# One 512-column product over both input parts in place of two of 256 columns, in a split-precision transformer trunk

## The chip, the cores and the metric

The kernel runs on one core of a Trainium2 chip, as one program. The metric is the device time of one execution in microseconds, median of several. TensorE (PE) does the products, VectorE (DVE) and ScalarE (ACT) read their sums out of PSUM, GpSimd (POOL) and the DMA queues do the rest.

## The reference

One inference step of a four-layer decoder trunk with a width of 1024, for 512 prompt tokens and 8 sample tokens that share all weights. Layers 0 and 3 mix tokens with a diagonal state space model (S5), layer 1 with stick-breaking attention, layer 2 with a chunked gMLP; after each mixer comes a SwiGLU feed-forward sub-layer with 2816 hidden columns, and around every sub-layer an RMS norm. Everything is float32.

```
for i in range(DEPTH):                        # 4
    xpn = rms_norm(xp, norm_mix_pre[i])       # and the same for the sample tokens
    op = mixer(xpn)                           # S5, attention, gMLP, S5
    xp = xp + rms_norm(op, norm_mix_post[i])
    h = rms_norm(xp, norm_ffn_pre[i])
    gate, up = jnp.split(h @ w_ffn_in[i], 2, axis=-1)
    xp = xp + rms_norm((jax.nn.silu(gate) * up) @ w_ffn_out[i], norm_ffn_post[i])
```

## The kernel before

Activations lie with features on the partitions and the 520 tokens (512 and 8) as columns. A dense product gives one output tile m of 128 features by 520 tokens, summed over k, the tiles of 128 input features (8 of them, or 6 in the first chunk of the feed-forward output). For precision near float32 each weight and each input is cut in two parts of type float32r: a high part (`wh`, `xh`), which ScalarE copies, and the low part that is left (`wl`, `xl`), a difference on VectorE or GpSimd. Three products are summed: wh by xh, wh by xl, wl by xh.

The 520 columns are two halves, HA = 256 and HB = 264. `mm` (line 225) issues one step of k: for each half the two products with `wh` (lines 231 and 232), then for each half the one with `wl` (line 234), so six products for both halves. The sums of an item lie in a pair of PSUM banks, a tile of 1024 columns from `pair`, of which there are three; HA goes to columns 256 to 511, the end of the first bank, HB to 512 to 775, the second.

`full` (line 245) goes over items (an item is one output tile m with a function that evicts it), both halves together, one item after the other or a group of two or three with k outside. Weights are loaded two items ahead: a DMA on the SP queue into `raw`, the cast to `wh` on ScalarE (line 207), the difference `wl` on VectorE (line 208). `split` (line 265) runs a sub-layer's first products (`lead`) and its last ones, one half after the other; it calls `mm` with one half. The last items of a feed-forward sub-layer and of attention's and gMLP's output are two in one group of `full` and then six in `split`.

Evictions: the feed-forward gate is lines 1551 to 1553, its up part line 1562 and then `hilo` (lines 379 and 380), its output line 1574; S5's gate is line 977 (sigmoid on ScalarE) and its value line 984; attention's q, k, v are lines 1341, 1350 and 1358; the output of attention and gMLP is lines 322 and 1409. In attention, line 1225 is a scan on VectorE. Two tasks use the ring `pn` of two buffers of 264 columns: `turn`, the norm between sub-layers, and attention's sample task, for its losses (`em`) and its sums (`accv`, lines 1130 to 1137).

The order of the work is written out by `pe`, which counts a modelled time of the products and lets waiting tasks in when they are due; on each engine a scheduler orders the instructions by this order and by what is ready.

## Time and profile before

| | |
|---|---|
| median of 3 runs | 2789.01 us (2787.88 to 2795.05) |
| span of the profiled execution | 2783.3 us |
| TensorE, weight loads | busy 2563.5 us (92%), 2458.0 us (88%) |
| VectorE | busy 1584.0 us (57%) |
| ScalarE | busy 1007.4 us (36%) |
| mean granted clock of TensorE | 0.953 |

The profile is one execution of the program on the chip. Its times are in us, those marked as a mean are ns; an engine is named PE, PEld (TensorE's weight loads), DVE, ACT, POOL or SP, and L231 is line 231 of the kernel. A row names what an instruction writes and reads, as out<-in. Products are pipelined: their durations overlap, so their pace is read from their starts.

### The profile page before, as it was taken

To read this page: it belongs to the slowest core of one execution; us is meant where nothing else is said; L and a number is where in the kernel's file an instruction comes from. 1 tells how busy PE (TensorE), PEld (TensorE's weight loads), DVE (VectorE), ACT (ScalarE), POOL (GpSimd) and SP (SyncE) were. 2 spreads that over 40 slices of the span, in tenths; PEclk is the share of its full clock that TensorE was granted. 3 is DMA by queue.
4 is the path that set the end of the run, shared out by engine and by line. 5 is a ranking of instruction groups with operands and counts; after the bars stand their busy time and mean duration, and the time that the engine had idled before them with its cause. 6 is when DMAs were issued, how large, how long until landed. Compare 5 with 4: busy or idle time off the path is not lost.

```text
span 2783.3 us, 49827 instructions
## 1 busy us (share of the span) xinstructions
PE 2563.5 (92%) x20826; PEld 2458.0 (88%) x20826; DVE 1584.0 (57%) x2668; ACT 1007.4 (36%) x1685; POOL 609.4 (22%) x598
## 2 busy tenths in 40 slices
PE   7769999999898889999998899999998679999998
PEld 6659999999886659999998899999997669999998
DVE  8883643434669975534347666443447864634344
ACT  5443432222346463332223534322223433432221
POOL 5661300000538821200003203000016640300000
PEclk8879999999899989999998999999998889999999
DMA  4533133332346742233324331333322514233331
GB/s 116 144 93 89 57 99 104 93 93 70 111 130 214 228 130 85 75 101 91 92 84 81 99 92 54 110 95 93 93 67 55 143 50 126 65 101 92 91 92 47
DMA packets 476544, 274.49 MB, mean 99 GB/s; under 512 B 51912, under 2 KB 458720, under 8 KB 476320
## 3 DMA queue, kind: packets, MB, share of 16 engines
q1 hardware_dynamic: 467104, 237.76, 30.3%
q0 software_dynamic: 9216, 33.56, 3.6%
q8 instruction: 164, 2.69, 0.4%
q14 instruction: 60, 0.49, 0.1%
HBM read 253.60 MB, written 17.66 MB: 97 GB/s over the span
## 4 chain that ended last, share of the span: by engine, by line
PE 68%; DVE 17%; DMA 3%; ACT 3%; issue 3%; POOL 2%; SPq 0%; ACTq 0%; DVEq 0%; POOLq 0%
PE pp L231 22%; PE pp L232 21%; PE pp L234 21%; DVE m L1225 2%; DVE wl L208 1%; DVE pn L409 1%; DVE x L411 1%; DVE hm L827 1%; DVE xl L394 1%; POOL kp L1089 1%; DVE o L817 1%; DVE zs L1092 1%; DMA rot<-rotd 1%; POOL x L411 1%; DVE o L815 1%
## 5 line engine op out<-in xcount | busy, mean ns | idle before, releaser
L231 PE MATMUL pp<-xh,wh 128*128 128x264 f32 (+1 forms) x4480 | 1217.4, 290 | 36.6 <-ACT xh L393 6.9
L232 PE MATMUL pp<-xl,wh 128*128 128x264 f32 (+1 forms) x4480 | 1216.8, 288 | 10.3 <-DVE xl L394 10.3
L234 PE MATMUL pp<-xh,wl 128*128 128x264 f32 (+1 forms) x4480 | 999.5, 287 | 13.5 <-POOL wl L208 7.4
L231 PEld LDWEIGHTS pp<-xh,wh 128*128 128x128 f32 x4480 | 860.1, 192 | 48.0 <-issue 18.2
L232 PEld LDWEIGHTS pp<-xl,wh 128*128 128x128 f32 x4480 | 861.3, 192 | 14.7 <-DVE xl L394 13.4
L207 ACT ACTIVATE wh<-raw 128x1024 fp32r<-128x1024 f32 (+1 forms) x376 | 390.5, 1042 | 1156.6 <-PE pp L232 873.7
L234 PEld LDWEIGHTS pp<-xh,wl 128*128 128x128 f32 x4480 | 745.1, 192 | 17.9 <-POOL wl L208 7.9
L208 DVE TENSOR_TENSOR wl<-raw,wh 128x1024 fp32r<-128x1024 f32 (+1 forms) x346 | 432.7, 1252 | 292.6 <-ACT wh L207 283.2
L232 PE MATMUL pp<-hl,wh 128*128 128x256 f32 (+1 forms) x1408 | 377.3, 283 | 0.0
L231 PE MATMUL pp<-hh,wh 128*128 128x256 f32 (+1 forms) x1408 | 376.0, 283 | 0.0
L234 PE MATMUL pp<-hh,wl 128*128 128x256 f32 (+1 forms) x1408 | 314.4, 282 | 0.0
L208 POOL TENSOR_TENSOR wl<-raw,wh 128x1024 fp32r<-128x1024 f32 x30 | 71.9, 2402 | 1050.6 <-ACT wh L207 1013.9
L232 PEld LDWEIGHTS pp<-hl,wh 128*128 128x128 f32 x1408 | 265.3, 188 | 0.0
L231 PEld LDWEIGHTS pp<-hh,wh 128*128 128x128 f32 x1408 | 265.0, 188 | 0.0
L234 PEld LDWEIGHTS pp<-hh,wl 128*128 128x128 f32 x1408 | 231.3, 188 | 0.0
L1551 DVE TENSOR_TENSOR tg<-pp,rs 128x520 f32<-128x520 f32 (+2 forms) x100 | 62.5, 631 | 236.6 <-PE pp L234 236.5
L1562 DVE TENSOR_TENSOR tg<-pp,tg 128x520 f32<-128x520 f32 (+2 forms) x96 | 62.6, 652 | 222.6 <-PE pp L234 222.0
L1574 DVE TENSOR_TENSOR op<-pp,op 128x520 f32<-128x520 f32 (+2 forms) x88 | 48.4, 550 | 191.9 <-PE pp L234 191.9
L326 POOL TENSOR_TENSOR acc<-acc,s 128x256 f32<-128x256 f32 (+1 forms) x96 | 83.3, 867 | 74.5 <-ACT s L322 72.5
L394 DVE SCALAR_TENSOR_TENSOR xl<-x,gt,xh 128x264 fp32r<-128x264 f32 (+1 forms) x128 | 86.5, 689 | 3.5 <-ACT xh L393 2.9
L393 ACT ACTIVATE xh<-x,gt 128x264 fp32r<-128x264 f32 (+1 forms) x128 | 62.7, 504 | 57.7 <-POOL x L411 33.4
L1070 POOL MEMSET zs<- 128x28 f32 x1 | 0.1, 121 | 339.3 <-PE pp L234 339.3
(332 smaller groups left out, 2879.1 us busy)
## 6 DMA issues: line engine op xcount, KB each, us to landing
raw<-in_w_ffn_in_dram SPq DMA_DIRECT2D x176, 512.0 KB, 3.8
raw<-in_w_ffn_out_dram SPq DMA_DIRECT2D x64, 512.0 KB, 3.9
raw<-in_w_ssm_glu_dram SPq DMA_DIRECT2D x32, 512.0 KB, 4.6
raw<-in_w_ffn_out_dram SPq DMA_DIRECT2D x32, 384.0 KB, 3.4
raw<-in_w_sb_qkv_dram SPq DMA_DIRECT2D x24, 512.0 KB, 4.1
raw<-in_w_ssm_in_dram SPq DMA_DIRECT2D x16, 512.0 KB, 4.4
wn<-dk SPq DMA_DIRECT2D x128, 64.0 KB, 2.5
raw<-in_w_cm_in_dram SPq DMA_DIRECT2D x16, 512.0 KB, 4.1
```

Source lines behind the costliest of these rows:

```text
L207: nc.scalar.activation(wh[:, :nk], raw[:, :nk], AF.Copy)
L208: (nc.gpsimd if self.edge & WLP else nc.vector).tensor_tensor(wl[:, :nk], raw[:, :nk], wh[:, :nk], op=ALU.subtract)
L231: nc.tensor.matmul(ps(*h), lhsT=wh[:, k, :], rhs=xh[:, h[0]:h[1]], start=first, stop=False)
L232: nc.tensor.matmul(ps(*h), lhsT=wh[:, k, :], rhs=xl[:, h[0]:h[1]], start=False, stop=False)
L234: nc.tensor.matmul(ps(*h), lhsT=wl[:, k, :], rhs=xh[:, h[0]:h[1]], start=False, stop=last)
L326: i = (nc.gpsimd if pool else nc.vector).tensor_tensor(acc[0][:, c0:c1], acc[0][:, c0:c1], sq[:, :n], op=ALU.add)
L393: nc.scalar.activation(xs[k][0][:, c0:c1], self.x[k][:, c0:c1], AF.Copy, scale=g)
L394: nc.vector.scalar_tensor_tensor(xs[k][1][:, c0:c1], self.x[k][:, c0:c1], g, xs[k][0][:, c0:c1], op0=ALU.mult, op1=ALU.subtract)
L411: add.tensor_tensor(self.x[k][:, c0:c1], self.x[k][:, c0:c1], t[:, :n], op=ALU.add)
L1225: v.tensor_tensor_scan(m[:, a:b][:, ::-1], m[:, a:b][:, ::-1], e[:, a:b][:, ::-1], 0.0, op0=ALU.add, op1=ALU.add)
L1551: v.tensor_tensor(g, ps(c0, c1), rs[:, c0:c1], op=ALU.mult)
L1562: v.tensor_tensor(t, ps(c0, c1), t, op=ALU.mult)
```

## The change

In `full`, and there alone, the two products of a step with `wh` on HA become one of 512 columns: its input is both parts of HA's 256 input columns (the low part first), its output the whole first bank, the low sum in columns 0 to 255 and the high sum in 256 to 511. The product with `wl` on HA adds to the high sum, as before. So a step has five products. When an item is done, ScalarE copies its low sum to a buffer of the ring `pn`, VectorE adds it to the high sum in PSUM, and the eviction follows as it was. To make both parts one input, `xh` and `xl` become the two halves of one tile of [128, 2, 520], and `hh` and `hl` as well. `split` still issues six products over two halves. The rest of the diff is comments.

```diff
-    def mm(self, ps, pc, k, x, halves, first, last):
+    def mm(self, ps, pc, k, x, halves, first, last, both=None):
         nc = self.nc
         wh, wl, _ = pc
-        xh, xl = x
+        xh, xl = x[:, 1], x[:, 0]
         for h in halves:
+            if both is not None and h == HA:
+                nc.tensor.matmul(both.rearrange("p (i c) -> p i c", i=2), lhsT=wh[:, k, :], rhs=x[:, :, h[0]:h[1]],
+                                 start=first, stop=False)
+                continue
             nc.tensor.matmul(ps(*h), lhsT=wh[:, k, :], rhs=xh[:, h[0]:h[1]], start=first, stop=False)
             nc.tensor.matmul(ps(*h), lhsT=wh[:, k, :], rhs=xl[:, h[0]:h[1]], start=False, stop=False)
...
-            pss = [self.pair()[1] for _ in g]
+            prs = [self.pair() for _ in g]
+            pss = [pr[1] for pr in prs]
             for k in range(nk):
-                for pc, ps in zip(pcs, pss):
-                    self.mm(ps, pc, k, get(k), (HA, HB), k == 0, k == nk - 1)
+                for pc, (t, ps) in zip(pcs, prs):
+                    self.mm(ps, pc, k, get(k), (HA, HB), k == 0, k == nk - 1, t[:, 0:512])
             self.leave(pcs)
+            for t, _ in prs:
+                cr = self.nrm.tile([128, 264], F32, tag="pn", name="cr")[:, :256]
+                self.nc.scalar.activation(cr, t[:, 0:256], AF.Copy)
+                self.nc.vector.tensor_tensor(t[:, 256:512], t[:, 256:512], cr, op=ALU.add)
             for it, ps in zip(g, pss):
                 it[3](ps, *FULL)
...
     def new_x(self):
-        return [(self.xnp.tile([128, N], F32R, tag="xh", name=f"xh{k}"),
-                 self.xnp.tile([128, N], F32R, tag="xl", name=f"xl{k}")) for k in range(KT)]
+        return [self.xnp.tile([128, 2, N], F32R, tag="xh", name=f"xh{k}") for k in range(KT)]
...
     def hilo(self, dst, src, c0, c1):
         nc = self.nc
-        nc.scalar.activation(dst[0][:, c0:c1], src, AF.Copy)
-        nc.vector.tensor_tensor(dst[1][:, c0:c1], src, dst[0][:, c0:c1], op=ALU.subtract)
+        nc.scalar.activation(dst[:, 1, c0:c1], src, AF.Copy)
+        nc.vector.tensor_tensor(dst[:, 0, c0:c1], src, dst[:, 1, c0:c1], op=ALU.subtract)
...
-                        hs[m] = (hp.tile([128, N], F32R, tag="hh", name="hh"),
-                                 hp.tile([128, N], F32R, tag="hl", name="hl"))
+                        hs[m] = hp.tile([128, 2, N], F32R, tag="hh", name="hh")
```

## Rows read from the trace of the kernel before

**Rows 1.** The page: the span, busy time by engine, the chain by line.
```profile
span 2783.3 us, 49827 instructions
...
PE 2563.5 (92%) x20826; PEld 2458.0 (88%) x20826; DVE 1584.0 (57%) x2668; ACT 1007.4 (36%) x1685; POOL 609.4 (22%) x598
...
PE pp L231 22%; PE pp L232 21%; PE pp L234 21%; DVE m L1225 2%; DVE wl L208 1%; DVE pn L409 1%; DVE x L411 1%; DVE hm L827 1%; DVE xl L394 1%; POOL kp L1089 1%; DVE o L817 1%; DVE zs L1092 1%; DMA rot<-rotd 1%; POOL x L411 1%; DVE o L815 1%
```

**Rows 2.** Stretches (attention; feed-forward): length, busy PE PEld DVE ACT POOL, clock, DMA.
```profile
770.00:1060.00 290.00, 250.86 (x1848) 193.74 (x1848) 236.00 (x294) 159.62 (x223) 162.27 (x144) 0.93 0.54 170
...
2415.00:2720.00 305.00, 305.00 (x2539) 305.00 (x2538) 126.51 (x148) 86.67 (x107) 0.00 (x0) 1.00 0.34 99
```

**Rows 3.** TensorE's waits from 320 to 700 us: total, times, longest.
```profile
PE pp L232 <- DVE xl L394: 1.5, 1, 1.5
PE pp L231 <- DVE tg L1551: 0.6, 1, 0.6
```

**Rows 4.** Timeline (start, duration): first product of two steps, eight steps apart.
```profile
600.05 0.28 PE L231 MATMUL pp<-xh,wh 128*128 128x256 f32 x1
...
605.83 0.28 PE L231 MATMUL pp<-xh,wh 128*128 128x256 f32 x1
```

**Rows 5.** Timeline of `split`, columns 256 then 264; below, that stretch's busy times.
```profile
676.13 0.28 PE L231 MATMUL pp<-hh,wh 128*128 128x256 f32 x1
...
687.06 0.28 PE L231 MATMUL pp<-hh,wh 128*128 128x256 f32 x1
...
701.09 0.29 PE L231 MATMUL pp<-hh,wh 128*128 128x264 f32 x1
...
707.31 0.29 PE L231 MATMUL pp<-hh,wh 128*128 128x264 f32 x1
...
676.00:708.00 32.00, 32.00 (x270) 32.00 (x269) 16.68 (x43) 8.91 (x21) 4.88 (x4) 1.00 0.18 50
```

**Rows 6.** Products by line and form: count, busy us, mean ns, idle before.
```profile
L231 PE MATMUL pp<-xh,wh 128*128 128x256 f32 x2240 | 646.6, 289 | 23.7 <-DVE op L1574 6.4 <-DVE g L1455 3.7 <-ACT wh L207 3.2
...
L231 PE MATMUL pp<-hh,wh 128*128 128x256 f32 x704 | 197.4, 280 | 0.0
```

**Rows 7.** Two lines' instructions: shortest, median and longest duration in ns.
```profile
L959 ACT ACTIVATE so<-pso x4: 369/374/378, 222.1 to 2296.4; 128x256 f32<-128x256 f32 x4
...
L1132 DVE TENSOR_TENSOR accv<-accv,psv x24: 382/412/422, 872.3 to 1034.3; 128x256 f32<-128x256 f32 x24
```

**Rows 8.** Timeline at the end of a gate item: ScalarE, then VectorE.
```profile
655.59 1.06 ACT L207 ACTIVATE wh<-raw 128x1024 fp32r<-128x1024 f32 x1 [4.14 <-PE pp L232]
...
655.83 0.70 DVE L1551 TENSOR_TENSOR tg<-pp,rs 128x520 f32<-128x520 f32 x1 [3.06 <-PE pp L234]
656.68 1.22 DVE L208 TENSOR_TENSOR wl<-raw,wh 128x1024 fp32r<-128x1024 f32 x1 [0.15 <-ACT wh L207]
```

**Rows 9.** Timeline at the end of S5's group of three: ScalarE, then TensorE.
```profile
239.70 1.28 ACT L977 ACT_TABLE_LOAD   x1
240.99 0.60 ACT L977 ACTIVATE sg<-pp 128x520 f32<-128x520 f32 x1
...
241.65 0.39 PE L231 MATMUL pp<-xh,wh 128*128 128x256 f32 x1 [1.16 <-ACT sg L977]
```

**Rows 10.** Timeline at the feed-forward's last group of two: ScalarE, then VectorE.
```profile
672.19 2.01 ACT L207 ACTIVATE wh<-raw 128x1024 fp32r<-128x1024 f32 x2 [9.20 <-PE pp L232]
...
672.43 1.42 DVE L1574 TENSOR_TENSOR op<-pp,op 128x520 f32<-128x520 f32 x2 [8.13 <-PE pp L234]
673.77 2.35 DVE L208 TENSOR_TENSOR wl<-raw,wh 128x1024 fp32r<-128x1024 f32 x2
```

**Rows 11.** TensorE's waits from 1060 to 1112 us, attention's output: the longest.
```profile
PE pp L231 <- DVE op L1409: 1.8, 1, 1.8
```

**Rows 12.** Attention (770 to 1060): the chain by line; the last instructions on `accv`.
```profile
by line: DVE m L1225 16.7%; issue 10.1%; POOL kp L1089 7.0%; DVE zs L1092 6.3%; DVE wl L208 6.2%; DVE z L1227 3.9%; DVE m L1222 3.6%; PE pp L231 3.2%; PE pp L234 3.2%; PE pp L232 3.1%; PE pp L1267 3.0%; ACT z L1228 2.4%; DMA raw<-in_w_sb_ou
...
L1137 DVE TENSOR_REDUCE sv<-accv x8: 586/598/607, 889.4 to 1035.2; 128x64 f32<-128x256 f32 x8
```

More of the change, by code (lines that the diff above doesn't have):

```diff
@@ L392, in pre_split1 @@
         g = self.gain(which, layer, k)
-        nc.scalar.activation(xs[k][0][:, c0:c1], self.x[k][:, c0:c1], AF.Copy, scale=g)
-        nc.vector.scalar_tensor_tensor(xs[k][1][:, c0:c1], self.x[k][:, c0:c1], g, xs[k][0][:, c0:c1],
+        nc.scalar.activation(xs[k][:, 1, c0:c1], self.x[k][:, c0:c1], AF.Copy, scale=g)
+        nc.vector.scalar_tensor_tensor(xs[k][:, 0, c0:c1], self.x[k][:, c0:c1], g, xs[k][:, 1, c0:c1],
                                        op0=ALU.mult, op1=ALU.subtract)
```

## The prediction

> **What bounds the kernel now.** I read the page's busy times first [rows 1]: TensorE is busy for 92% of the span, VectorE for 57%, ScalarE for 36%. A share over the whole span says nothing of a single stage, so the table of stretches comes next [rows 2]. In the last feed-forward sub-layer's stretch TensorE is busy for all of 305.00 us while VectorE has 126.51 and ScalarE 86.67: there only products count. In the attention stretch VectorE is busy for 236 of 290 us and TensorE for 251: a product saved there is not always saved time. The list of waits then says how tight the dense stretch is: in the 380 us of the first feed-forward sub-layer TensorE waits twice, for 2.1 us in all [rows 3]. So every nanosecond taken from the stream of products of a feed-forward sub-layer should come off the end. The chain of waits agrees: the three product lines make 22 + 21 + 21% of it [rows 1].
>
> **Where a product's time goes.** Durations of single products overlap (0.28 us each, a new one every 0.12 us), so the start-to-start time is what counts. One step of k (six products) starts at 600.05, the ninth at 605.83: 8 steps in 5.78 us, 0.7225 us a step, 120.4 ns a product [rows 4]. A stretch that has products of 256 columns alone shows 31 steps of three from 676.13 to 687.06: 117.5 ns each; one with 264 alone, 17 steps from 701.09 to 707.31: 122.0 ns [rows 5]. The granted clock is 1.00 over both [rows 5], the 2.4 GHz level, at which 256 and 264 columns stream in 106.7 and 110.0 ns. What is left is 10.8 and 12.0 ns: a fixed part of 11.4 ns for each product, whatever its columns. It isn't the weight load that sets the pace, or both would start equally far apart.
>
> **What is removed.** In `full`, two products of 256 columns with the same weights become one of 512. The columns stay, one fixed part goes. Lines 231 with 256 columns count 2240 + 704 = 2944 steps [rows 6]; by the code 2272 of them are in `full` (feed-forward 4 x (39 x 8 + 8 x 6 + 8 x 8 + 2 x 8) = 1760, S5 2 x 14 x 8 = 224, attention 22 x 8 = 176, gMLP 14 x 8 = 112). Where TensorE is the bound I count all of feed-forward and gMLP, S5's gate products (160) and attention's output products (16): 2048 x 11.4 ns = 23.3 us. The other 224 steps, S5's input products and attention's q, k, v, fill gaps of other chains: 0 to 2.6 us, taken at 0, as TensorE idles there anyway. No row shows a one-pass product of 512 columns. Its bounds: 213.3 ns (512 columns at 2.4 GHz and no fixed part), which saves 235.0 - 213.3 = 21.7 ns a step or 44 us; and twice 117.5 ns, if the two pieces of its input are each begun anew, which saves nothing. I take 213.3 + 11.4 = 224.7 ns, since rows 5 show a part that goes with the instruction.
>
> On this the Trainium skill speaks against the change: "TensorE: Matmul & The Clock Gate", section "Back-to-back issue gap", gives the warm distance as the columns at 2.4 GHz and 2.5 ns; by that figure the same removal would be an estimated 2048 x 2.5 ns = 5 us. The trace does not agree for these products: 117.5 ns stands [rows 5] where the Trainium skill has 109.2.
>
> **What is added.** Each of the 292 items of `full` (57 x 4 + 28 + 22 + 14) gets a ScalarE copy of 256 columns from PSUM (0.374 us, line 959) and a VectorE add of 256 (0.412 us, line 1132, one input in PSUM; no row writes its result to PSUM, the row is the nearest) [rows 7]: 0.79 us more between the last product and the eviction, 120 us of VectorE and 109 us of ScalarE in all.
>
> In feed-forward this is covered. An item takes about 5.8 us; its buffer pair is one of three, so it must be empty when the third next item starts, 11.5 us after its own last product. At the end of an item ScalarE's weight cast starts at 655.59, the eviction at 655.83 [rows 8]. The copy will queue behind that cast (to 656.65), the add perhaps behind the weight difference of line 208 (656.68 to 657.90); the eviction then ends near 659, 8 us before the pair is wanted. Queued behind the waiting add on VectorE are differences of weights that TensorE reads an item or two later, behind the waiting copy on ScalarE the next silu or split: free too. With VectorE at 126.51 of 305.00 us [rows 2], its some 53 more adds (305.00 us at 5.8 us an item) are 22 us of 178 idle. Were the cover gone, it would cost up to 228 x 0.79 = 180 us; nothing in the rows comes near. The inputs of the output products need the last split two items (11 us) later, also covered.
>
> Where the eviction is waited for, it costs:
> - S5's first three gate products run as one group and fill all three pairs. TensorE then waits 1.16 us for the sigmoid, whose 1.28 us table load runs ahead, from 239.70, while the products still run (they end 1.16 before 241.65) [rows 9]. After the change ScalarE is held by the copy, which waits for the products, and the load comes after it: copies and add about 0.8 us, load and sigmoid 1.9 us, less what is waited now. From 0.8 us (the load stays early) to 2.7; I take 1.8, twice: 3.6.
> - The end of a feed-forward sub-layer: two items end together, and the first product of the second item of `split` wants the first one's pair 2.8 us later (3 x 8 x 117.5 ns). ScalarE has two weight casts from 672.19 to 674.20, VectorE the evictions at 672.43 and differences from 673.77 to 676.1 [rows 10]. With the copies behind the casts and the adds behind the differences, the first pair is free at about 677, 2 us late; with the copies first there is no wait. 0 to 2, I take 0.5, four times: 2.0.
> - Output products of attention and gMLP, the same group of two: attention's wait for this eviction is 1.8 us already [rows 11], so the 0.79 lies on the path: 0.8 to 2, I take 1.0, twice: 2.0.
> - Attention: 20 items, 8.2 us of VectorE where VectorE's lines head the chain [rows 12]. From 0 (in its idle 54 us) to 8.2; I take 3.0, as line 1225 alone is 17% of the chain there and scattered waits leave room.
> - S5's inputs, 8 items ahead of a long VectorE chain: 0 to 3, I take 0.5.
>
> Sum of costs 11.1 us (3.6 + 2.0 + 2.0 + 3.0 + 0.5), bounds 3.2 and 28.6. The two input parts now share a tile: the first product waits for both parts, which the second did 0.12 us later, so nothing. No DMA is moved. The sum: -23.3 + 11.1 = -12.2 us. The profiled execution has a span of 2783.3, 5.7 under the median of 2789.0; the difference lies outside the stream of products and stays. 2789.0 - 12.2 = 2776.8.
>
> **Rivals.**
> 1. The long product hides its fixed part (213.3 ns): 44 us less, 11.1 more, 2756. For: a longer stream leaves the next weight load more time. Against: 256 and 264 columns already differ by the columns alone [rows 5], so the load is hidden now. Chance 0.12. With the 2.5 ns of the same section of the Trainium skill on the long product alone, an estimate gives 2761.
> 2. The evictions cost close to their upper bounds (casts ahead of the copies in all six groups of two, the late table load, nearly all of attention's adds on the chain): 24 of 28.6 us against 23.3 gained, about 2790, at most 2794. For: ScalarE's casts are released just before the last products of an item [rows 8, 10]. Chance 0.17.
> 3. No gain from the long product: it streams two pieces of input, each with its own fixed part, and takes 235 ns. Then only the costs are left: 2789 + 11 = 2800. It decides from 230 ns on (10 us gained). For: its input jumps by 520 elements in the middle. The Trainium skill's section named above, 2.5 ns a product in place of 11.4, comes to much the same, an estimated 2789 - 5 + 11 = 2795. Chance 0.08. This is also the case in which the change doesn't do what it says.
> 4. Slower by a new wait: the copy takes its buffer from the ring `pn` of two, in which attention's `accv` sums sit one after the other, eight of them; the last reduction of the first starts at 889.4, that of the eighth at 1035.2 [rows 12], 20.8 us apart, and the first's adds start at 872.3 [rows 7], so each sits for about 18 us. If slots are handed out strictly in turn, the second copy of each k, v pair waits for a sum to end, about 9 us; some five pairs fall there, 45 us, of which perhaps 27 on the path: 2804. It decides when a copy waits over 5 us. Against: one slot is free most of the time. Chance 0.08.
>
> **How the numbers follow.** Forecast case 0.55 (2776.8, its own range 2770 to 2785), rivals 0.12, 0.17, 0.08, 0.08. A measurement of this kernel tells 0.3%, 8.4 us, from no change, so faster means under 2780.6. Of the forecast case 0.43 lies below that and 0.12 within; rival 1 is faster, rival 2 the same, rivals 3 and 4 slower: faster 0.55, same 0.29, slower 0.16. Range 2756 to 2794: it reaches to rivals 1 and 2 and leaves out 3 and 4.
>
> **What would show it.** A feed-forward step of five products every 0.711 us instead of 0.7225, the next start 225 ns after the long one (213 for rival 1, 235 for rival 3). The dense stretch still with TensorE busy throughout, each feed-forward sub-layer 5 us shorter. TensorE's wait for the sigmoid near 3 us. Waits of the first product for lines 1574 and 1409 at the group's end. In attention, copies that wait for a sum would show rival 4. The forecast is wrong if the pitch of the 512-column product is not near 225 ns, or if TensorE shows idle time inside the feed-forward stretches.

## The result, and the profile after

The change makes the kernel slower: 2821.68 us (2819.47 to 2823.71) against 2792.03 us of the kernel before on the same chip, a ratio of 1.0106 with a 95% interval of 1.0085 to 1.0128. The prediction was 2776.8, with a range to 2794. The profiled execution has a span of 2822.0 us, 38.7 more than before's 2783.3; the medians are 29.7 apart. A time on record exceeds its span by about 2 us, so the profiled execution of before took some 2785 us (an estimate), 7 under the 2792.03, and the sections below are measured against it.

The page of the kernel after, to be held against [rows 1]: span, busy time by engine, the chain by line. All line numbers behind `mm` have moved by 5 to 10: 231, 232 and 234 are now 236, 237 and 239, the new product is line 233, the copy 270, the add 271.

```profile
span 2822.0 us, 46054 instructions
...
PE 2558.8 (91%) x18554; PEld 2347.6 (83%) x18554; DVE 1706.3 (60%) x2960; ACT 1104.1 (39%) x1977; POOL 609.9 (22%) x598
...
PE pp L239 21%; PE pp L233 17%; PE pp L236 13%; PE pp L237 13%; DVE m L1235 2%; DVE wl L208 1%; DVE hm L837 1%; DVE pn L419 1%; DVE x L421 1%; DVE xh L404 1%; ACT wh L207 1%; DVE o L827 1%; DVE o L832 1%; POOL x L421 1%; DVE o L831 1%
```

VectorE has 122 us more work and ScalarE 97, as the added passes make it, and TensorE has 2272 fewer instructions. None of that says where 39 us come from. One line followed through both traces does: the 376 weight casts of line 207 are the same in every kernel, and how far a cast starts behind its twin of before shows where the time is lost. Sections between casts, in us gained (-) or lost (+) against the profiled execution of before; the three columns on the right are kernels of the experiments:

| section (cast numbers) | before's time at its end | after | e1_other_ring | e3_ffn_gmlp | e14_s2_held |
|---|---|---|---|---|---|
| start, first S5 (to 36) | 376.2 | +4.4 | +5.2 | -1.5 | +3.6 |
| feed-forward 1 (36 to 88) | 655.6 | -1.9 | -2.5 | -2.0 | -4.6 |
| attention and its output (88 to 132) | 1144.6 | +37.6 | +22.9 | -6.8 | +2.8 |
| feed-forward 2 (132 to 180) | 1396.6 | -2.6 | -2.4 | -2.7 | -1.4 |
| gMLP (180 to 228) | 1748.3 | -3.5 | -3.2 | -0.3 | +0.7 |
| feed-forward 3 (228 to 276) | 2008.1 | -3.4 | -3.5 | -3.1 | -3.5 |
| second S5 (276 to 312) | 2360.8 | +9.0 | +8.5 | +1.8 | +5.7 |
| feed-forward 4 (312 to 372) | 2710.4 | -2.8 | -2.9 | -3.0 | -2.9 |
| sum | | +36.8 | +22.1 | -17.6 | +0.4 |

So the dense sub-layers gain, a little over half of what was predicted; the two S5 layers lose 13.4 us; and attention alone loses 37.6.

The dense stretch first. Timeline of TensorE in the kernel after (start, duration), to be held against [rows 4]: a long product, the product behind it, and the long product eight steps later; below, the stretch of the last feed-forward sub-layer (length, busy times, granted clock), which answers to [rows 2].

```profile
600.28 0.39 PE L233 MATMUL pp<-xh,wh 128*128 128x512 f32 x1
600.51 0.28 PE L236 MATMUL pp<-xh,wh 128*128 128x264 f32 x1
...
606.00 0.39 PE L233 MATMUL pp<-xh,wh 128*128 128x512 f32 x1
```
```profile
2447.00:2752.00 305.00, 305.00 (x2137) 286.06 (x2137) 150.91 (x206) 106.41 (x165) 2.41 (x1) 1.00 0.34 98
```

Eight steps take 5.72 us, 715 ns each, where before took 722.5. The next product starts 0.23 us behind the long one; over 249 such pairs of the first feed-forward sub-layer the mean is 232.3 ns. TensorE is busy for all of 305.00 us, with VectorE at 151 and ScalarE at 106: the passes are hidden there.

The attention stretch, from the first load of a q, k, v weight to the first of the next sub-layer (length, busy PE, PEld, DVE, ACT, POOL, clock), before and after:

```profile
675.00:1062.50 387.50, 338.27 (x2496) 276.15 (x2496) 293.58 (x433) 197.06 (x292) 199.29 (x189) 0.93 0.48 152
```
```profile
676.90:1101.50 424.60, 345.56 (x2315) 269.96 (x2315) 310.85 (x457) 204.84 (x314) 201.65 (x189) 0.90 0.45 139
```

It is 37 us longer, though VectorE has only 17 us more to do and ScalarE 8. TensorE has 181 fewer products and yet 7 us more busy time: the granted clock fell from 0.93 to 0.90, while TensorE is idle for 79 us of the stretch where before has 49.

### The profile page after: what moved, and what is told of

It reads as the page before. It is cut to its first block, busy times and chain, and to the rows that moved or that the text cites. A ratio compares the mean times of both kernels' runs of the same rounds, so it can differ in the third digit from the quotient of the medians.

```text
span 2822.0 us, 46054 instructions
## 1 busy us (share of the span) xinstructions
PE 2558.8 (91%) x18554; PEld 2347.6 (83%) x18554; DVE 1706.3 (60%) x2960; ACT 1104.1 (39%) x1977; POOL 609.9 (22%) x598
## 4 chain that ended last, share of the span: by engine, by line
PE 68%; DVE 17%; issue 4%; DMA 3%; ACT 3%; POOL 2%; SPq 1%; ACTq 0%; DVEq 0%; POOLq 0%
PE pp L239 21%; PE pp L233 17%; PE pp L236 13%; PE pp L237 13%; DVE m L1235 2%; DVE wl L208 1%; DVE hm L837 1%; DVE pn L419 1%; DVE x L421 1%; DVE xh L404 1%; ACT wh L207 1%; DVE o L827 1%; DVE o L832 1%; POOL x L421 1%; DVE o L831 1%
## 5 line engine op out<-in xcount | busy, mean ns | idle before, releaser
L236 PE MATMUL pp<-xh,wh 128*128 128x264 f32 (+1 forms) x2720 | 786.8, 291 | 23.9 <-DVE op L1583 6.5
L237 PE MATMUL pp<-xh,wh 128*128 128x264 f32 (+1 forms) x2720 | 787.4, 290 | 10.2 <-DVE xh L404 10.2
L233 PE MATMUL pp<-xh,wh 128*128 128x512 f32 x1760 | 704.7, 400 | 20.9 <-ACT sg L987 6.5
L237 PEld LDWEIGHTS pp<-xh,wh 128*128 128x128 f32 x2720 | 525.8, 193 | 93.2 <-DVE xh L404 12.9
L236 PEld LDWEIGHTS pp<-xh,wh 128*128 128x128 f32 x2720 | 525.3, 194 | 28.9 <-ACT xh L403 8.3
L233 PEld LDWEIGHTS pp<-xh,wh 128*128 128x128 f32 x1760 | 334.3, 190 | 28.9 <-issue 11.9
L236 PE MATMUL pp<-hh,wh 128*128 128x264 f32 (+1 forms) x896 | 253.8, 283 | 4.4 <-DVE op L1583 4.4
L237 PE MATMUL pp<-hh,wh 128*128 128x264 f32 (+1 forms) x896 | 253.5, 283 | 0.0
L233 PE MATMUL pp<-hh,wh 128*128 128x512 f32 x512 | 201.8, 394 | 0.0
L237 PEld LDWEIGHTS pp<-hh,wh 128*128 128x128 f32 x896 | 168.5, 188 | 22.6
L236 PEld LDWEIGHTS pp<-hh,wh 128*128 128x128 f32 x896 | 168.5, 188 | 5.1 <-issue 5.1
L271 DVE TENSOR_TENSOR pp<-pp,cr 128x256 f32<-128x256 f32 x292 | 124.0, 426 | 14.9 <-ACT cr L270 14.7
L389 ACT ACTIVATE hh<-tg 128x520 fp32r<-128x520 f32 (+2 forms) x96 | 57.7, 601 | 171.7 <-DVE tg L1571 171.6
L1562 ACT ACTIVATE sg<-tg 128x520 f32<-128x520 f32 (+2 forms) x100 | 58.0, 585 | 154.7 <-DVE tg L1561 154.6
L270 ACT ACTIVATE cr<-pp 128x256 f32<-128x256 f32 x292 | 107.5, 368 | 13.0 <-PE pp L239 8.5
```

The source lines that it names most:

```text
L233: nc.tensor.matmul(both.rearrange("p (i c) -> p i c", i=2), lhsT=wh[:, k, :], rhs=x[:, :, h[0]:h[1]], start=first, stop=False)
L236: nc.tensor.matmul(ps(*h), lhsT=wh[:, k, :], rhs=xh[:, h[0]:h[1]], start=first, stop=False)
L237: nc.tensor.matmul(ps(*h), lhsT=wh[:, k, :], rhs=xl[:, h[0]:h[1]], start=False, stop=False)
L270: self.nc.scalar.activation(cr, t[:, 0:256], AF.Copy)
L271: self.nc.vector.tensor_tensor(t[:, 256:512], t[:, 256:512], cr, op=ALU.add)
L389: nc.scalar.activation(dst[:, 1, c0:c1], src, AF.Copy)
```

## The experiments

Medians and ratios to the kernel before on the same chip, and the length of the attention stretch in the profiled execution. A "wide product" is the one of 512 columns with its copy and add. The runs lie on several chips, so from row to row the ratios compare better than the times. e4_ruler leaves columns of the low part out, ran once (2750.3 us) and serves for the pace alone.

| kernel | us | ratio, 95% interval | attention |
|---|---|---|---|
| e1_other_ring | 2802.3 | 1.0039 (1.0023 to 1.0054) | 410.5 |
| e2_no_attn | 2801.0 | 1.0034 (1.0011 to 1.0057) | 386.9 |
| e3_ffn_gmlp | 2767.7 | 0.9918 (0.9896 to 0.9940) | 382.5 |
| e5_tile_only | 2796.1 | 1.0034 (1.0017 to 1.0050) | 388.7 |
| e6_attn | 2797.8 | 1.0041 (1.0026 to 1.0056) | 411.0 |
| e7_s5 | 2785.7 | 1.0011 (0.9993 to 1.0028) | 384.8 |
| e8_attn_dve | 2796.5 | 1.0034 (1.0021 to 1.0047) | 408.0 |
| e9_attn_passes | 2794.1 | 1.0026 (1.0007 to 1.0046) | 409.7 |
| e10_attn_wide_only | 2784.1 | 0.9972 (0.9954 to 0.9990) | 394.5 |
| e11_attn_held | 2782.2 | 0.9985 (0.9962 to 1.0007) | 392.5 |
| e12_order_alone | 2797.3 | 1.0025 (1.0007 to 1.0043) | 415.3 |
| e14_s2_held | 2786.9 | 1.0000 (0.9986 to 1.0013) | 388.3 |
| e15_s2_held3 | 2786.0 | 0.9989 (0.9974 to 1.0004) | 388.3 |
| e16_s5_held | 2780.9 | 0.9978 (0.9961 to 0.9995) | 382.6 |
| e17_e3_held | 2779.0 | 0.9959 (0.9935 to 0.9983) | 398.9 |
| e18_before_other_order | 2786.8 | 0.9997 (0.9986 to 1.0009) | 385.5 |

The last column is one execution each. Where q, k and v have no wide product and no passes (before, e2, e3, e5, e7, e16, e17, e18) it reads 382.5 to 398.9, so a difference of less than some 16 us in it can't be told from one profile; the ratios decide there.

### The ring of the copies

The prediction's rival 4: copies that wait for the ring `pn`. The trace of after has two copies that follow closely on the last reduction on an `accv` sum, which gives its buffer of the ring back. ScalarE and VectorE, in order of time:

```profile
936.72 0.62 DVE L1147 TENSOR_REDUCE sv<-accv 128x64 f32<-128x256 f32 x1
...
936.94 1.06 ACT L1233 ACTIVATE e<-e 128x1024 f32<-128x1024 f32 x1
...
937.91 0.37 ACT L270 ACTIVATE cr<-pp 128x256 f32<-128x256 f32 x1
...
997.53 0.61 DVE L1147 TENSOR_REDUCE sv<-accv 128x64 f32<-128x256 f32 x1
...
998.04 0.84 ACT L1250 ACTIVATE z<-pp,abias 128x256 f32<-128x256 f32 x2
...
998.77 0.39 ACT L270 ACTIVATE cr<-pp 128x256 f32<-128x256 f32 x1
```

A sum ends at 937.34 and at 998.14, and a copy starts 0.6 us behind each. But ScalarE stands in neither place: it works on the instruction ahead of the copy until 938.00 and 998.88. Its waits ahead of copies in the whole attention stretch (total us, times, longest) are few, and one of them, 0.6 us, is for a sum:

```profile
ACT cr L270 <- DVE pp L271: 2.1, 1, 2.1
...
ACT cr L270 <- PE pp L239: 0.8, 2, 0.5
...
ACT cr L270 <- DVE sv L1147: 0.6, 1, 0.6
```

So the sign that rival 4 gave for itself, a copy that waits over 5 us, isn't there. e1_other_ring takes the copy's buffer from another ring.

```diff
-                cr = self.nrm.tile([128, 264], F32, tag="pn", name="cr")[:, :256]
+                cr = self.nrm.tile([128, 264], F32, tag="s2", name="cr")[:, :256]
```

> The change, with the copy's buffer taken from the ring `s2` (two buffers of 264 columns, which only the norms' squares use) in place of `pn`. The eviction's copy, add and products stay. From the first load of attention's weights to the first load of the next feed-forward weights the kernel before takes 387.5 us, the changed one 424.6. Theory A, the ring shared with `accv` makes the copies and the sums wait for each other: the stretch falls to 388 to 397 us (what stays is the copies' and adds' own work) and the time to 2785 to 2795. Theory B, the copies and adds themselves, in a stretch where VectorE is nearly full, lengthen it: it stays above 415 us, the time above 2812.

Measured: 2802.3 where the change has 2821.7, ratio 1.0039 for 1.0106, and an attention stretch of 410.5, between theory A's and theory B's. So the choice of the ring is worth 19 us; the two profiled executions are 15 us apart, 14 of them in the attention stretch. How the ring costs this is not shown. The other ring also comes with another order of the old instructions: in the attention section of the two traces 90 of VectorE's 582, copies and adds left out, stand elsewhere (matched by operation, tiles and form). Rival 4 named the right buffer, the waits that it described are not what the trace shows, and it was not the whole loss.

### One part of the change at a time

e2_no_attn gives attention's q, k and v items their six products back. e3_ffn_gmlp has the wide product only in items of feed-forward and gMLP that run one by one, with the ring `s2`; e6_attn adds attention's items to that, e7_s5 S5's. All by a flag at the calls of `full`, as here for e2:

```diff
-            self.full(kvi[m], xs, KT, nxt=items[10 + 2 * m:])
+            self.full(kvi[m], xs, KT, nxt=items[10 + 2 * m:], wide=False)
```

> The change everywhere but in attention's q, k and v products, which run as before (six products a step, no copy, no add); ring `pn` as in the change. Either theory gives a stretch of 385 to 390 us and a time of 2783 to 2790, as long as attention's loss lies in these items. Against the kernel with the other ring it tells what the copies and adds cost in attention by themselves: 0 by theory A in its pure form, up to 8 us (20 adds of 0.42) if they lie on the chain, over 25 by theory B.

> The wide product in the feed-forward and gMLP items of `full` that run one by one only; S5, attention and the groups of two ahead of a `split` as before; copy in ring `s2`. A feed-forward step fell from 722.3 to 714.7 ns, 7.6 ns; 424 steps in each of four sub-layers give 12.9 us, gMLP's 96 another 0.7. Theory A, the losses lie in the waits for evictions at the groups' ends, in S5 and in attention, and this keeps the gain alone: 2775 to 2780. Theory B, the copies and adds cost time in the dense stretches as well, or the shared tile of both input parts does: 2784 or above.

> The feed-forward and gMLP form (2767.7 us; 382.5 us from attention's first weight load to the next feed-forward one) with the wide product, copy and add in attention's q, k and v as well, copy in ring `s2`. Theory A, the ring shared with `accv` was the whole of attention's loss: 2766 to 2776, the stretch up to 392. Theory B, copies and adds cost by themselves there, beside the ring: 2783 to 2795, the stretch above 400, as in the profile of the change with the other ring (410.5).

> The feed-forward and gMLP form (2767.7 us) with the wide product in both S5 layers as well, input and gate products. By the waits alone: the group of three waits 3.3 instead of 1.2 us for the sigmoid, twice, 4.2 us; 224 steps x 7.6 ns gain at most 1.7: theory A, 2769 to 2773. Theory B, the input items' later evictions push the VectorE chain that follows (the changed kernel lost 5.5 and 8.2 us by the end of its two S5 layers), so 10 us or more: 2778 to 2785.

e2's executions scatter from 2781.9 to 2807.6 us. Its median of 2801.0 lies outside the 2783 to 2790 that was expected and settles little; its profiled execution (2786.2) has attention back at 386.9, and where the longer ones lose their time no profile shows. e3 beats both kernels: 2767.7, ratio 0.992, below what theory A gave. Against e3, attention's 20 items cost 30 us (e6) and S5's 18 (e7), as theory B had it for both, or slightly more; by the ratios it is 34 and 26.

e5_tile_only keeps all six products and only puts both input parts into one tile, which the prediction had priced at nothing.

```diff
-                    self.mm(ps, pc, k, get(k), (HA, HB), k == 0, k == nk - 1, t[:, 0:512])
+                    self.mm(ps, pc, k, get(k), (HA, HB), k == 0, k == nk - 1, None)
...
-            for t, _ in prs:
+            for t, _ in ():
```

> Both input parts share a tile, as in the change, but every step runs six products as before, with no copy and no add. Theory A, the shared tile costs and gains nothing, and the 21 us that the feed-forward and gMLP form is faster than before are all its products' (13.6 us by 1792 steps x 7.6 ns) and run-to-run spread: 2784 to 2793. Theory B, part of that gain comes with the tile, through another order of the instructions: 2775 to 2783.

Two starts eight steps apart in e5_tile_only, against [rows 4]:

```profile
599.75 0.28 PE L236 MATMUL pp<-xh,wh 128*128 128x256 f32 x1
...
605.60 0.28 PE L236 MATMUL pp<-xh,wh 128*128 128x256 f32 x1
```

731 ns a step here; over 246 steps the mean is 726.8 where before has 722.2. 2796.1 lies above what either theory gave. The layout alone makes a step 4.6 ns slower where `xh` is the input and 2.1 ns where `hh` is, and the kernel 0.34%. Another order of the instructions is not the reason: in the two traces VectorE and ScalarE take their instructions in the same sequence. What the reason is, no run asked.

### The pace of the long product

e4_ruler gives the long product another width in each feed-forward sub-layer, once as one run of columns (line 236) and once as two pieces (line 239).

```diff
-                nc.tensor.matmul(both.rearrange("p (i c) -> p i c", i=2), lhsT=wh[:, k, :], rhs=x[:, :, h[0]:h[1]],
-                                 start=first, stop=False)
+                if kind == 1:
+                    nc.tensor.matmul(both[:, :w], lhsT=wh[:, k, :], rhs=x.rearrange("p i n -> p (i n)")[:, :w],
+                                     start=first, stop=False)
+                else:
+                    nc.tensor.matmul(both[:, :w].rearrange("p (i c) -> p i c", i=2), lhsT=wh[:, k, :],
+                                     rhs=x[:, :, 0:w // 2], start=first, stop=False)
```

> A measurement of the long product's pace, with copy ring `s2`. From the second step of an item on, the wide product of a feed-forward item takes other columns: in layer 0 one piece of 512 (input) and one of 448 (output), in layer 1 two pieces of 256 and two of 224, in layer 2 one of 384 and one of 320, in layer 3 two of 192 and two of 160. Its sums are not those of the reference: the one-piece forms read other columns of the low part, the short forms leave columns out. Theory A, each piece of the input has its own fixed part of 11.4 ns and columns cost 0.417 ns: next start 225 and 198 ns after one piece of 512 and 448, 171 and 145 after 384 and 320, and 7 to 11 ns more where there are two pieces. Theory B, the pace is linear in the columns with a larger price for each, 0.445 ns and 4 ns fixed (a line through 118 at 256 and 232 at 512): 232, 203, 175 and 146 ns, with no difference between one piece and two.

Products of e4_ruler by line and form (count, busy us, mean ns of one):

```profile
L236 PE MATMUL pp<-xh,wh 128*128 128x384 f32 x273 | 92.2, 338 | 0.0
L239 PE MATMUL pp<-xh,wh 128*128 128x384 f32 x273 | 92.2, 338 | 0.0
L239 PE MATMUL pp<-hh,wh 128*128 128x448 f32 x96 | 35.1, 366 | 0.0
L236 PE MATMUL pp<-hh,wh 128*128 128x448 f32 x96 | 35.1, 365 | 0.0
L236 PE MATMUL pp<-hh,wh 128*128 128x320 f32 x96 | 29.7, 310 | 0.0
L239 PE MATMUL pp<-hh,wh 128*128 128x320 f32 x96 | 29.7, 310 | 0.0
```

Two pieces cost what one costs, at a granted clock of 1.00. From start to next start the means are 147 ns at 320 columns, 175 at 384, 204 at 448 and 232 at 512, with 117.5 at 256 from [rows 5]: some 28.5 ns for every 64 columns, that is 0.445 ns a column and 4 ns for the product, as theory B had it. The timeline shows the same step from 448 to 512:

```profile
440.05 0.36 PE L236 MATMUL pp<-hh,wh 128*128 128x448 f32 x1
440.25 0.28 PE L242 MATMUL pp<-hh,wh 128*128 128x264 f32 x1
...
440.74 0.39 PE L236 MATMUL pp<-hh,wh 128*128 128x512 f32 x1
440.97 0.28 PE L242 MATMUL pp<-hh,wh 128*128 128x264 f32 x1
```

### Attention: passes, product, or order

With the ring gone, 23 to 28 us were left in attention (e1 against before, e6 against e3). First theory: ScalarE's copy waits in line. e8_attn_dve moves attention's copies to VectorE.

```diff
+                if dve:
+                    self.nc.vector.tensor_copy(cr, t[:, 0:256])
+                else:
+                    self.nc.scalar.activation(cr, t[:, 0:256], AF.Copy)
```

> The same as the form with attention's items, but in attention VectorE does the copy too, so that ScalarE, which is in the middle of the chain of exponentials, never waits for a product there. 8.2 us more work for VectorE, 7.5 less for ScalarE. Theory A, attention's loss comes from ScalarE standing at a copy that waits for TensorE: the stretch shrinks against the form with ScalarE's copy, by 5 us or more. Theory B, VectorE's time is what counts: it grows by 5 to 10 us. No difference if the loss is the ring's alone.

408.0 for 411.0, less than the 5 us that either theory asked for: ScalarE's line was not it. What VectorE waits for looked odd, though. Its waits in the attention stretch (total us, times, longest), first before, then after:

```profile
DVE wl L208 <- ACT wh L207: 20.5, 8, 6.4
...
DVE zs L1092 <- POOL kp L1089: 3.5, 4, 1.2
```
```profile
DVE wl L208 <- ACT wh L207: 36.3, 13, 6.3
DVE zs L1102 <- POOL kp L1099: 19.1, 6, 6.3
```

VectorE waits 31 us more for weight casts and for GpSimd's products with cached pages, and neither is part of the change. An instance from the timeline of VectorE in the kernel after:

```profile
851.16 1.22 DVE L1102 TENSOR_REDUCE zs<-kp 128x16 f32<-128x1024 f32 x1 [6.26 <-POOL kp L1099]
852.30 0.69 DVE L1368 TENSOR_TENSOR v<-pp,rs 128x520 f32<-128x520 f32 x1
```

Directly ahead of the eviction of v stands a reduction that waits 6.26 us for GpSimd, and the eviction doesn't pass it: it starts behind the reduction, at 852.30. Which of the two comes first is worked out by a scheduler when the kernel is built, from modelled times. New instructions change those times, so old instructions come out in another order. By a count in the built programs, 229 of VectorE's 2670 common instructions stand elsewhere in e6_attn than in e3_ffn_gmlp; in the attention section of the traces, matched as above, it is 119 of 582.

Four runs tell the passes, the product and the order apart. e9 has six products and adds two passes that change nothing; e10 has the wide product and no passes; e11 has the whole change in attention, but with the instructions of four engines held in e3's order; e12 is e3, held in e6's order. The order is held by edges between neighbours, from a list of numbers:

```diff
+    for d, n in zip(nums[::2], nums[1::2]):
...
+                if last is not None:
+                    tc.add_manual_dep(mine[q], last.name, mybir.DependencyInfo(
+                        mybir.DependencyClass.NoSync, mybir.DependencyReason.DATA), reason="order")
+                last = mine[q]
```

> Base is the version with the wide product in feed-forward and gMLP alone (ratio 0.992 to before, attention stretch 382.5 us in its profile). Here attention's q, k, v items (20 of the 22 that run without halves) keep their six products, and each gets a copy of 256 columns from PSUM on ScalarE and a VectorE pass of 256 columns back into PSUM (the maximum of the sum and its own copy, which leaves it as it is): the two passes without the wide product. Theory P (the two passes hold the PSUM pair and the in-order VectorE longer): attention stretch 404 to 411 us, ratio 0.999 to 1.005. Theory W (the wide product itself disturbs attention, not the passes): 381 to 387 us, ratio 0.990 to 0.995. Theory O (neither as such, but the order of the instructions on each engine, which the scheduler works out anew when an instruction is added): between the two, since this program has an order of its own, with about as many instructions out of place as the version with the whole change in attention.

> The same base; attention's q, k, v items take the wide product, and neither the copy nor the add follows (the products with the input's low part are left out of the first 256 columns of q, k and v). Theory P: attention stretch 379 to 384 us, ratio 0.990 to 0.994. Theory W: 404 to 411 us, ratio 0.999 to 1.005. Theory O: near P's, 380 to 388, since few instructions stand elsewhere than in the base (57 of VectorE's 2670 against 229 in the version with the whole change in attention).

> The whole change in attention (wide product, copy in the other ring, add), 411.0 us and ratio 1.004 before; but the instructions of TensorE, VectorE, ScalarE and GpSimd in the attention stretch are held in the order in which they stand in the base, the copies and adds joining where they are ready. Theory P: the passes stay, so 404 to 411 us and a ratio of 0.999 to 1.005. Theory O: the order was what cost, so 382 to 390 us and a ratio of 0.991 to 0.996. Theory W: as P.

> The base itself (six products, no copy, no add in attention) with the instructions of the four engines in the attention stretch held in the order in which they stand in the version with the whole change there. Theory P and theory W: nothing is added, so 380 to 386 us and a ratio of 0.990 to 0.995. Theory O: the order alone costs, so 400 to 411 us and a ratio of 0.998 to 1.005. If both order and passes count, this one and the one before share the 28 us between them.

The attention stretch of e3, e6, e11 and e12, in this order:

```profile
671.40:1053.90 382.50, 337.57 (x2486) 275.17 (x2485) 293.72 (x432) 197.38 (x291) 200.48 (x189) 0.93 0.49 154
```
```profile
676.00:1087.00 411.00, 342.32 (x2328) 270.46 (x2327) 303.69 (x453) 202.91 (x312) 198.17 (x189) 0.90 0.46 143
```
```profile
672.40:1064.90 392.50, 338.71 (x2327) 267.89 (x2326) 294.89 (x453) 203.31 (x312) 197.90 (x189) 0.93 0.48 150
```
```profile
670.50:1085.80 415.30, 345.14 (x2485) 279.98 (x2484) 292.48 (x433) 197.15 (x291) 199.61 (x189) 0.89 0.46 142
```

e12 shows that order by itself can cost this much. It has the instructions of e3, none added (VectorE's busy time is 292 us, e3's 294), and the other order alone makes the stretch 33 us longer and the kernel 29.6; its ten executions (2794.0 to 2802.4) lie clear of e3's six (2762.2 to 2779.8). In the attention section its trace has e6's sequence of old instructions on VectorE and ScalarE, and e11's has e3's, without exception. Nor is it the holding: e18 below, a whole program held, is at 0.9997.

e11 has all of the added work, and in e3's order the stretch is 18.5 us shorter than e6's. What is left for product and passes is 10 us by the stretch and 19 by the ratios (0.9985 against 0.9918); the profiled execution is 4.5 us under e11's median. That is more than the 0 to 7.5 that theory O left them, and the ratio lies between theory O's and theory P's: the order is part of attention's loss, the passes are another. e9 (409.7, 1.0026) comes out as theory P had it, but it has an order of its own, so it can't tell passes from order. e10's 394.5 lies within what one profile can't tell, from an execution 7.8 us over its median; its ratio, 0.9972, is 15 us above e3's, between the ranges of theory P and theory W. That wasn't followed further. VectorE's waits follow, e3 first, then e12, then e11, where the adds (line 274) wait for their copies more than for anything else and the stretch still is the shorter one:

```profile
DVE wl L208 <- ACT wh L207: 15.5, 9, 6.2
...
DVE zs L1102 <- POOL kp L1099: 4.0, 4, 1.2
```
```profile
DVE wl L208 <- ACT wh L207: 41.5, 14, 6.9
DVE zs L1102 <- POOL kp L1099: 19.2, 7, 5.9
```
```profile
DVE pp L274 <- ACT cr L273: 30.8, 14, 5.2
DVE wl L209 <- ACT wh L208: 14.7, 5, 6.6
```

And e12 shows the scene of the kernel after once more, with no added instruction in sight; the last line is TensorE's, whose 6.23 us of idle time that eviction ends:

```profile
842.71 1.22 DVE L1102 TENSOR_REDUCE zs<-kp 128x16 f32<-128x1024 f32 x1 [5.89 <-POOL kp L1099]
843.97 0.70 DVE L1368 TENSOR_TENSOR v<-pp,rs 128x520 f32<-128x520 f32 x1
...
844.72 2.08 PE L1218 MATMUL pp<-kz,q 128*128 128x512 f32 x2 [6.23 <-DVE v L1368]
```

e8's stretch stays open: it is 408 us long, yet VectorE waits only 16.8 us for casts; there the copies themselves wait 13.3 us for TensorE.

### The order over the whole program

e14_s2_held is the whole change with the ring `s2`, held over the whole program in the order of before; e15_s2_held3 the same in e3's order; e16_s5_held is e7 in e3's order. The edit is the one above.

> The whole change with the copy's buffer in the other ring (2802 us, ratio 1.004, attention stretch 410.5 us), with the instructions of TensorE, VectorE, ScalarE and GpSimd held over the whole program in the order in which the kernel before has them; copies and adds join where they are ready. Theory O (the order that the scheduler works out anew costs most of the time): attention stretch 387.5 plus the 10 us that the passes cost in a held order, 397 us; the S5 stretches within 3 us of before each; 2786 to 2793 us, ratio 0.999 to 1.003. Theory P (the passes cost it): attention 405 to 411, S5 5 to 8 us longer each, ratio 1.003 to 1.006.

> The same kernel held in the order of the base (wide product in feed-forward and gMLP alone, 2768 us, attention stretch 382.5). Theory O: attention stretch near 393 us, 2778 to 2787 us, ratio 0.996 to 1.000. Theory P: attention 405 to 411, ratio 1.003 to 1.006.

> The base with the wide product in S5's input and gate products too (free order: ratio 1.001; its weight casts in the feed-forward sub-layer behind the first S5 stand 6.7 us behind the base's, behind the second S5 another 8 us), held in the order of the base. Theory O for S5: those 6.7 and 8 us shrink to at most 2 to 3 us each, 2768 to 2775 us, ratio 0.992 to 0.995. Theory P for S5 (the wait for the sigmoid, 3.3 us for 1.2, and the passes ahead of the long VectorE chain): they stay at 5 to 8 us each, ratio 0.998 to 1.002.

In before's order the whole change, ring apart, comes out at 1.0000 (0.9986 to 1.0013), where the same instructions in the scheduler's order (e1) have 1.0039: 11 us by the ratios, 15 by the medians. Attention loses 2.8 us there in place of 22.9, less than the 10 that theory O had allowed for the passes; e15 (0.9989, 388.3) comes out as theory O had it too. S5 is another matter. e14 loses 3.6 and 5.7 us there, where theory O allowed 3 each, and e16, against e3, still loses 6.3 us up to the first feed-forward sub-layer and 4 around the second S5 (casts 276 to 312), where free e7 loses 6.6 and 8; its ratio of 0.9978 lies between what the two theories gave. There the theory of the order fails for the first layer and holds for half of the second; what remains in a held order lies with the wide product and its passes. The change as it stands, with the ring `pn`, wasn't tried in a held order, so how much of the ring's 19 us is waiting for a buffer and how much another order stays open.

Last, how much of e3's gain is the wide product, and how much its order. e17_e3_held is e3 in before's order, e18_before_other_order is before in e3's.

> The base (wide product in feed-forward and gMLP alone, ratio 0.992 in its free order) held over the whole program in the order of the kernel before. If the base's gain is the wide product's alone, it stays: ratio 0.991 to 0.993. If part of it is the order that the scheduler happened to find (its attention stretch, in which nothing is changed, is 5 us shorter than before's), the attention stretch goes back to 387 us, and the ratio is 0.993 to 0.996 (four feed-forward sub-layers of 3.4 us and some 1 us of gMLP, 14.6 us of 2789).

> The kernel before, no part of the change, held in the order of the base. If the order is worth the 5 us: attention stretch 382 to 384 us, ratio 0.997 to 0.999. If not: 387 us and 1.000.

e18 gives 0.9997 (0.9986 to 1.0009): e3's order by itself is worth nothing that can be told. e17 gives 0.9959 (0.9935 to 0.9983), in the range of the case in which part of e3's gain is its order. With before's order 11 of e3's 21 to 23 us remain, which is what e3's four feed-forward sections add up to in the table (10.8 us). But its executions scatter from 2761.2 to 2788.8, and the profiled one (2779.5) lost 17.6 us against before's between casts 104 and 116, in attention, where apart from the shared tile neither instructions nor order differ from before. So attention's length also varies from one execution to the next. e17 speaks for the order and e18 against it, so where the other half of e3's gain comes from is open. It bears on e11 too: against e17's ratio in place of e3's, product and passes cost 7 us there and not 19.

## Why the prediction was wrong, by its steps

From the predicted -12.2 us to the measured +29.7 it is 42 us. Roughly, 19 are the ring (e1) and 11 the order (e14 against e1), neither of them in the prediction's sum. The other 12 are terms of the sum that were mis-sized, read from the sections of e14: the feed-forward sub-layers gain 12.4 us where the sum had 18.1 (20.1 less 2.0), and the S5 layers lose 9.3 where it had 2.3 (4.1 less 160 products at 11.4 ns).

**The pace.** The step that failed is the reading of [rows 5]: 117.5 and 122.0 ns less the columns at 2.4 GHz gave a "fixed part" of 11.4 ns. Two widths 8 columns apart can't tell a fixed part from a dearer column: the difference that was read as fixed is mostly 0.028 ns on each of 256 columns (0.445 in place of 0.417), and 4 ns are fixed. So the long product takes 232 ns where 224.7 was predicted; it saves 3 ns against two starts of [rows 5], not 11.4, and 5 against the two that it replaces in the dense stretch (119.2 and 118.3). A whole feed-forward step saves 7.1 to 7.4 ns (714.8 for 722.2, 712.5 for 719.6), as the other four products come 2 ns closer too; against the same tile layout (e5) it saves 9 to 12. That is near the predicted 11.4, but by luck: only 4 to 5 of it are at the long product, and the rest is that the four other products stand closer together than in e5, which the prediction doesn't have and no run explains. The 1760 feed-forward steps, 20.1 us of the predicted 23.3, are worth 12.8 at that saving, and the four sections of after show 10.7 net. Rival 3 put its turning point at 230 ns, and the pace came out just past it, though for a reason of the columns and not of the two pieces, which cost nothing (e4).

The Trainium skill, "TensorE: Matmul & The Clock Gate", section "Back-to-back issue gap", has the columns at 2.4 GHz and 2.5 ns, for an isolated product. The prediction set it aside on [rows 5]; its small fixed part was nearer to the measured 4 ns than the 11.4, while its 215.8 ns for 512 columns lies 16 under the measured 232.

**The shared tile** was priced at nothing, since nothing waits for it. Right as to waits, wrong as to pace: 2 to 4.6 ns a step (e5).

**Feed-forward's cover** held: TensorE is busy throughout, and its waits from 322 to 702 us are 3.6 us, where [rows 3] have 2.1.

```profile
PE pp L237 <- DVE xh L404: 1.8, 1, 1.8
PE pp L236 <- DVE op L1583: 1.1, 1, 1.1
PE pp L236 <- DVE tg L1561: 0.7, 2, 0.6
```

The middle one is the group of two at the sub-layer's end, taken at 0.5 and bounded by 2. The output of attention waits 1.8 us for its eviction, as in [rows 11], where 1.0 more was expected. The copy (0.367 us) and the add (0.425 us, its result in PSUM) cost what [rows 7] gave.

**S5.** The late table load came as described: copies, then the load, then the sigmoid, and TensorE waits 3.3 us where [rows 9] have 1.2. ScalarE and TensorE of after:

```profile
243.18 0.38 ACT L270 ACTIVATE cr<-pp 128x256 f32<-128x256 f32 x1 [0.87 <-DVE pp L271]
243.59 1.28 ACT L987 ACT_TABLE_LOAD   x1
...
245.54 0.50 PE L233 MATMUL pp<-xh,wh 128*128 128x512 f32 x1 [3.26 <-ACT sg L987]
```

That is 2.1 us where 1.8 was taken (the prediction's own terms, 0.8 and 1.9 less 1.2, give 1.5). The input items were taken at 0.5 (bounds 0 and 3): held in e3's order, e16 is 3.0 us behind e3 when the first layer's gates begin (cast 12) and 4.1 four casts on. The term was mis-sized.

**Attention.** The step that failed stands nowhere in the prediction: it priced 20 copies and adds at 3.0 us, as if every engine kept the order it had, and the section came out 37.6 us longer. Held in before's order (e14) it is 2.8 longer, as priced; held in e3's (e11), the stretch is 10 us longer than e3's, above the bound of 8.2, and by the ratios more. What cost beside the ring is that the scheduler put old instructions elsewhere: 22.9 us in e1 for 2.8 in e14, and 33 us with no work added in e12.

**Rival 4** had the buffer and a size, 27 us on the path for 19 measured, and a chance of 0.08. Its reason against itself, "one slot is free most of the time", was given too much weight. The size is luck as far as the record goes: the second copy of each k, v pair was to wait about 9 us, and in the trace of after the copies wait 0.6 us for a sum in all.

**The 5.7 us** between the span of [rows 1] and the median were put outside the stream. In the runs that have both, about 2 us lie outside; the rest is that the profiled execution lay under the median. The sum doesn't depend on it.

## What to carry to other kernels

When a program's order is worked out by a scheduler, an edit anywhere in a stage with several busy engines is two changes, the work and the new order; compare the order of the built programs first, and hold it to price the work alone. Put new passes where one engine is the bound and the others are half idle (e3), into pipelines of several engines only with the order held (e1 against e14). A cost per column and one per instruction need widths that are far apart; 256 and 264 can't tell them from each other.

## What the runs showed of the hardware

- Products of type float32r at a granted clock of 1.00 start 117.5 ns apart at 256 columns, 147 at 320, 175 at 384, 204 at 448 and 232 at 512 ([rows 5], e4): 0.445 ns a column plus 4 ns. An input in two pieces costs no more than one in one.
- Putting both input parts into one tile, the high part 2080 bytes behind the low one, slows a step of six products by 2.1 ns (`hh`) to 4.6 ns (`xh`); the products of `xh` with 264 columns and `wl` go from 120.7 to 124.7 (e5). The cause is open.
- In attention, TensorE's idle time and its granted clock went together: 45 to 55 us idle with 0.93 (before, e3, e11, e14, e18), 63 to 79 us with 0.89 or 0.90 (after, e1, e6, e8, e9, e12). e12 has e3's products and 7.6 us more busy time (345.14 for 337.57), so there idle time was paid for a second time.
